# Ten gathered rows moved from ahead of the expert loop to its last quarter, and TensorE's tiles placed at one remainder of 512 bytes

## The chip, the core and the metric

The kernel runs on one core of a Trainium2 chip. The metric is the device time of one execution in microseconds (us). Besides the median of several runs there is one profiled execution, whose trace says when every instruction of every engine started and ended. The engines are named as the profile names them: PE (TensorE's matmuls; PEld are its weight loads), DVE (VectorE), ACT (ScalarE), POOL (GpSimd) and SP, which here only issues DMAs.

## What is computed

One encoder layer over 512 tokens of 1024 values: an input projection, two kinds of attention, an output projection, a layer norm, and then a mixture of 16384 very small experts (PEER) beside a gated embedding. The part that the change moves is PEER:

```python
q   = (xb @ w_q).reshape(128, 8, 256)            # per chunk of 128 tokens
...                                              # two top-16 lists per head, 16 best sums of them
idx = (e1 * 128 + e2).reshape(128, 8 * 16)       # 128 experts per token
g   = softmax(cv)                                # their weights
u   = u_table[idx]                               # 128 x 128 rows of 1024
hpre = einsum('td,ted->te', xb, u)
act  = g * gelu(hpre)
out  = einsum('te,ted->td', act, v_table[idx])
```

## The kernel before

Matmuls of 32-bit values are made from three products: an operand is cut into a high part and a low part (`split`, L103 to L110: ACT copies the high part, DVE subtracts to get the low one), and `mm3` (L120 to L123) adds high x high, high x low and low x high into the same PSUM tile. L121, L122 and L123 are therefore most of TensorE's lines, whatever they compute. In a row of the trace `acc<-v_hi,a_hi` the first operand after the arrow is the one that streams (512 or 256 columns), the second is the one that is loaded as weights (128 columns).

**PEER is done in two ways.** For the first 128 tokens (one per partition) the rows of the two tables are gathered: for each of 128 experts, POOL issues an indirect DMA of 128 rows of 4 KB, and one DVE instruction multiplies them with the tokens and sums (the u rows), or multiplies by a weight and adds to `base` (the v rows). For the other 384 tokens the whole tables go through TensorE: 128 blocks of 128 experts, with a dense weight matrix that is zero except where an expert was chosen.

**Ahead of the loop** (from about 417 us) stand the routing and the building of that matrix. All engines' orders are written out by hand here. DVE's order is the backbone: `route` makes the lists of experts of a chunk of 128 tokens, `build_g` (L887 to L960) makes the weight matrix of a chunk in 16 steps of one-hot masks (`oh`, L936) and weighted masks (`ow_hi`, `ow_lo`, L947), which TensorE multiplies (L914). There are three builds; the last is that of chunk 1 (`build_g(NGC, *held)`, L1202). Among DVE's steps stand gathered rows (`rows`, L962 to L970): 128 u rows of chunk 1 (operand `h_s`) until the second build, then, in the third build, the first `BESIDE` u rows of chunk 0 (L1205, operand `h`); `OWN_G` (L1207) sets how many rows go with a step of the build. Then `SOME` rows of chunk 0 that were fetched ahead, and on to `PRE` (L1315, L1322).

TensorE works there through 104 **lead blocks** (`lead_block`, L1026 to L1042): 512 KB of the u table are loaded (`raw`) and multiplied with 256 tokens (`whole`) in 8 matmuls of plain 32-bit values, each of which the trace shows as two. They are interleaved with DVE's steps by an account: `run_pe` (L878 to L885) adds a step's cost times `PACE` to `due`, and takes so many matmuls of the lead blocks as `due` covers.

**The loop** (L1337 to L1388, from about 918 us) goes over 128 blocks of the v table. Of each block n DVE makes the low part (`v_lo`, or `wlo` for odd n), of each second block also the low part of the weights (`a_lo`) and one product (L1361), and then its share of the gather steps; TensorE does 18 matmuls of 512 columns (`acc`, three chunks x two halves x three products). In the first 22 blocks a further block of the u table goes through TensorE (`expert_in`, 24 products of 256 columns, `hp<-hTh,whi`). Odd blocks from n = 25 keep their parts in a pool of the weights' streams (`whi`, `wlo`), even ones in the loop's own pool (`v_hi`, `v_lo`): that is why their names alternate in the trace. DVE and SP have orders written out by hand in the loop; TensorE's order there is the scheduler's.

`room(n)` (L1326 to L1329) says how many gather steps block n gets, as shares: all 257 steps of chunk 0 (128 u rows, one activation, 128 v rows) less the `PRE` that stand ahead are shared out in proportion.

A tile's place in SBUF follows from the pools: a pool begins where the one below it ends. `even` (L94 to L98) only puts a small tile into a pool so that what comes after it starts further up.

Of the kernel before, what the change touches and what calls it, by code (L numbers as in the profile page):

```python
# [9 lines left out]
F32 = mybir.dt.float32  # L10
# [26 lines left out]
WIDE = 40  # L37
LEAD = 104
SPILL = 72
FIRST = 8  # L40
PACE = 1.07
AHEAD = 14.0
LAG = 6.0
PRE = 41
SOME = 4
EARLY = 15
EARLY_AT = 4
BESIDE = 31
OWN = 1.0
OWN_G = 0.85  # L50
OWN_SOON = 1.2
HALF = 10
OT = 8
# [9 lines left out]
CLOSE = 31  # L63
# [13 lines left out]
def tile_encoder_layer(ctx: ExitStack, tc: tile.TileContext, A: dict, out: bass.AP):  # L77
    nc = tc.nc


    keep = ctx.enter_context(tc.tile_pool(name="keep", bufs=1))
# [9 lines left out]
    eps_t = keep.tile([128, 1], F32, name="eps_t")  # L91
    nc.vector.memset(eps_t, EPS)

    def even(pool):  # L94

        nc.vector.memset(pool.tile([128, 8], F32, name="even"), 0.0)

    even(keep)  # L98

    def r32(ap):  # L100
        return ap.bitcast(F32)
# [70 lines left out]
    turned = pT.enter_context(tc.tile_pool(name="turned", bufs=1, side="right"))  # L172
    hTh = turned.tile([128, 8, T], F32R, name="hTh")
    hTl = turned.tile([128, 8, T], F32R, name="hTl")
    even(turned)


    pA = ExitStack()
    at = pA.enter_context(tc.tile_pool(name="at", bufs=1))
# [17 lines left out]
    gk = at.tile([128, 2], F32, name="gk")  # L197
    ones = at.tile([128, 128], F32, name="ones")
    nc.vector.memset(ones, 1.0)

    def transpose_to(dst_h, dst_l, src, c):

# [445 lines left out]
    pB = ctx.enter_context(tc.tile_pool(name="pB", bufs=1, reuse_waits="tile"))  # L648
# [5 lines left out]
    h_split = None  # L654
    ge_ring = pB.tile([128, GES, 2, N_U], F32, name="ge_ring")
    ge_free = [ge_ring[:, j] for j in range(GES)]
    w_top = pB.tile([128, 2], F32, name="w_top")
    even(pB)

    def expert_in(i):  # L660

# [10 lines left out]
    rt = pR.enter_context(tc.tile_pool(name="rt", bufs=1, reuse_waits="tile"))  # L672
# [20 lines left out]
    v_all = rt.tile([128, 4, 8, 2, 16], F32, name="v_all")  # L693
    i_all = rt.tile([128, 4, 8, 2, 16], U32, name="i_all")
    s_ix = rt.tile([128, 128], I32, name="s_ix")
    even(rt)
    held = []
    rw = pR.enter_context(tc.tile_pool(name="rw", bufs=1, reuse_waits="tile"))
    h_s = rw.tile([128, D], F32, name="h_s")
# [178 lines left out]
    def run_pe(amount):  # L878
        nonlocal due
        due += amount * PACE  # L880
        while due > 0:
# [162 lines left out]
    def on_vector(share, f):  # L1044
        def task():
            nonlocal due
            f()
            due += share * PACE
        return task
# [128 lines left out]
    with tc.manual_schedule(engines={nc.vector.engine, nc.scalar.engine, nc.tensor.engine, nc.sync.engine,  # L1178
# [27 lines left out]
        own_due = 0.0  # L1206
        run(build, OWN_G)  # L1207
        for x in own:
# [27 lines left out]
    for j, (n, nb, _, _) in enumerate(g_tiles[1:], 1):  # L1236
        for c in range(NDC):
            at = n - 6 + c if nb == GB and n < WIDE else n - 4 + c // 2 if n == WIDE else n - 13 + 3 * c
# [65 lines left out]
    with tc.manual_schedule(engines={nc.vector.engine, nc.scalar.engine, nc.tensor.engine, nc.sync.engine,  # L1304
# [14 lines left out]
        for n in range(2):  # L1319
            v_cut[n] = cut_v(n)  # L1320
            blocks_ahead(1)
        for k in range(BESIDE + SOME, PRE):  # L1322
            gather_u(0, k)
        for _ in pe_work:
            pass
    def room(n):  # L1326
        if n < NO_GATHER or n > 124:
            return 0.0
        return 2.2 if n + LEAD < 126 else 1.6 if n < CLOSE else 1.0 if n < WIDE else 1.42 if n < 112 else 1.9  # L1329

    rooms = sum(room(n) for n in range(128))
    done, spent = PRE, 0
    with tc.manual_schedule(engines={nc.vector.engine, nc.sync.engine}):
# [157 lines left out]
```

## Time and profile before

| | |
|---|---|
| median of 3 runs | 1530.96 us (1530.82 to 1531.17) |
| the profiled execution | 1532.45 us |
| its span, first to last instruction | 1530.6 us |
| mean granted TensorE clock | 0.992 |
| instructions | 21801 |

The span is read best in five stretches: the projections and both attentions (0 to about 312 us), the queries and their scores (312 to 417), the lead blocks with routing and builds (417 to about 918), the loop's first blocks with `expert_in` (to about 1075), and the rest of the loop (to about 1519), behind which only the closing layer norms stand. A busy share is a sum over a stretch; since matmuls overlap in the records (one of 512 columns lasts 0.39 us but the next starts some 0.23 us later), what a matmul costs is read from the distance between starts, not from its duration.

### The profile page before, as it was taken

The page shows a single profiled execution, that of the slowest core. Times are in us where ns is not written, and L with a number is a line of the kernel's source. Part 1 is how long each engine was busy: PE and PEld are TensorE (multiplying, and loading weights), DVE is VectorE, ACT ScalarE, POOL GpSimd, SP SyncE. Part 2 cuts the span into 40 slices and gives each one's busy share as a digit, 9 for nine tenths or more (in the row PEclk, how much of TensorE's full clock was granted, in tenths as well). Part 3 has the DMA queues.
Part 4 walks back from the last instruction along what each step waited for, and adds up shares of the span by engine and source line. Part 5 has one row for each costly group of instructions (what it writes and reads, how often), then busy time and mean ns, then how long its engine had stood idle before and what let it go on. Part 6 is the DMA issues. An engine that isn't in the chain of part 4 may idle for free.

```text
span 1530.6 us, 21801 instructions
## 1 busy us (share of the span) xinstructions
PE 1464.4 (96%) x7715; PEld 1221.4 (80%) x7715; DVE 1272.0 (83%) x2639; ACT 543.2 (35%) x893; POOL 626.8 (41%) x537
## 2 busy tenths in 40 slices
PE   6999999999999999999899989999999999999996
PEld 4788777788887788887788878888788888888885
DVE  7276795658999897998889947988788999999998
ACT  3255785333322223222212223443333333333333
POOL 1013110043344344464415345655545555555560
PEclk9999999999999999999999999999999999999999
DMA  7233341194377899999979999999999999999992
GB/s 237 66 107 87 97 125 42 44 304 144 113 234 255 306 400 343 414 399 411 409 298 414 413 387 392 392 395 330 331 391 397 401 398 398 402 395 400 395 347 109
DMA packets 188414, 456.15 MB, mean 298 GB/s; under 512 B 16400, under 2 KB 80272, under 8 KB 185232
## 3 DMA queue, kind: packets, MB, share of 16 engines
q1 hardware_dynamic: 121264, 211.45, 38.6%
q0 software_dynamic: 58400, 208.69, 36.3%
q10 hardware_dynamic: 8640, 34.61, 5.6%
q8 instruction: 61, 1.00, 0.3%
q14 instruction: 49, 0.40, 0.1%
HBM read 413.01 MB, written 38.80 MB: 295 GB/s over the span
## 4 chain that ended last, share of the span: by engine, by line
PE 62%; DVE 13%; issue 10%; DMA 7%; POOL 5%; ACT 1%; SPq 0%; POOLq 0%; DVEq 0%; ACTq 0%
PE acc L121 10%; PE acc L123 10%; PE acc L122 10%; PE mm L1036 5%; DMA raw<-in_uT_dram 4%; PE pj L121 3%; PE pj L122 3%; PE pj L123 3%; PE mm L121 2%; PE mm L123 2%; PE mm L122 2%; POOL whi L966 2%; POOL row L966 2%; POOL wlo L966 2%; PE hp L121 1%
## 5 line engine op out<-in xcount | busy, mean ns | idle before, releaser
L1036 PE MATMUL mm<-whole,raw 128*128 128x256 f32 x1136 | 260.0, 385 | 8.5 <-DMA raw<-in_uT_dram 8.1
L1272 POOL DMA_INDIRECT gat<-in_v_rows_dram,i_sel x128 | 192.3, 1503 | 143.8 <-DVE base L1274 119.9
L1036 PEld LDWEIGHTS mm<-whole,raw 128*128 128x128 f32 x1136 | 213.3, 192 | 40.8 <-DMA raw<-in_uT_dram 7.8
L1257 POOL DMA_INDIRECT gat<-in_u_rows_dram,i_sel x97 | 149.4, 1540 | 119.2 <-DVE gat L1263 91.0
L121 PE MATMUL acc<-v_hi,a_hi 128*128 128x512 f32 x456 | 179.2, 393 | 3.7 <-ACT a_hi L106 2.4
L122 PE MATMUL acc<-v_lo,a_hi 128*128 128x512 f32 x456 | 178.8, 392 | 0.8 <-DVE v_lo L107 0.8
L123 PE MATMUL acc<-v_hi,a_lo 128*128 128x512 f32 x456 | 178.4, 392 | 0.6 <-DVE a_lo L107 0.6
L106 ACT CAST whi<-raw 128x1024 fp32r<-128x1024 f32 (+4 forms) x103 | 102.7, 997 | 199.4 <-PE acc L123 110.1
L1274 DVE SCALAR_TENSOR_TENSOR base<-gat,hdot,base 128x1024 f32<-128x1024 f32 x128 | 165.0, 1289 | 1.8
L107 DVE TENSOR_TENSOR wlo<-raw,whi 128x1024 fp32r<-128x1024 f32 (+4 forms) x103 | 118.6, 1152 | 47.0 <-ACT whi L106 46.2
L106 ACT CAST v_hi<-v_raw 128x1024 fp32r<-128x1024 f32 x76 | 79.8, 1051 | 174.4 <-issue 71.8
L1263 DVE SCALAR_TENSOR_TENSOR gat<-gat,h 128x1024 f32<-128x1024 f32 x97 | 115.0, 1218 | 10.9 <-DMA gat<-in_u_rows_dram,i_sel 10.9
L123 PE MATMUL acc<-whi,a_lo 128*128 128x512 f32 x312 | 123.0, 394 | 0.0
L122 PE MATMUL acc<-wlo,a_hi 128*128 128x512 f32 x312 | 123.0, 394 | 0.0
L121 PE MATMUL acc<-whi,a_hi 128*128 128x512 f32 x312 | 122.5, 394 | 0.0
L107 DVE TENSOR_TENSOR v_lo<-v_raw,v_hi 128x1024 fp32r<-128x1024 f32 x76 | 92.6, 1218 | 28.3 <-ACT v_hi L106 27.8
L121 PEld LDWEIGHTS acc<-v_hi,a_hi 128*128 128x128 f32 x456 | 85.9, 188 | 22.6 <-ACT a_hi L106 2.8
L123 PEld LDWEIGHTS acc<-v_hi,a_lo 128*128 128x128 f32 x456 | 86.0, 189 | 20.1 <-DVE a_lo L107 1.5
L122 PEld LDWEIGHTS acc<-v_lo,a_hi 128*128 128x128 f32 x456 | 86.0, 189 | 18.8 <-DVE v_lo L107 1.1
L966 POOL DMA_INDIRECT row<-in_u_rows_dram,s_ix x42 | 52.7, 1255 | 69.8 <-DVE row L968 44.2
L966 POOL DMA_INDIRECT wlo<-in_u_rows_dram,s_ix x43 | 52.3, 1217 | 68.8 <-DVE wlo L968 55.1
L966 POOL DMA_INDIRECT whi<-in_u_rows_dram,s_ix x43 | 53.9, 1253 | 57.9 <-DVE whi L968 36.9
(395 smaller groups left out, 3370.9 us busy)
## 6 DMA issues: line engine op xcount, KB each, us to landing
raw<-in_uT_dram SPq DMA_DIRECT2D x110, 512.0 KB, 7.4
v_raw<-in_v_rows_dram SPq DMA_DIRECT2D x78, 512.0 KB, 13.1
raw<-in_v_rows_dram SPq DMA_DIRECT2D x50, 512.0 KB, 13.7
g_dram<-g_st ACTq DMA_DIRECT2D x24, 1024.0 KB, 9.5
ge_dram<-ge_ring ACTq DMA_DIRECT2D x36, 256.0 KB, 7.3
g_wide<-g_dram SPq DMA_DIRECT2D x9, 1024.0 KB, 16.8
raw<-in_w_in_dram SPq DMA_DIRECT2D x17, 512.0 KB, 4.0
raw<-in_w_q_dram SPq DMA_DIRECT2D x16, 512.0 KB, 4.3
```

The lines of the kernel that those rows point to most:

```text
L106: nc.scalar.copy(hi, src)
L107: nc.vector.tensor_tensor(lo, src, r32(hi), op=OP.subtract)
L121: nc.tensor.matmul(ps, a[0], b[0], start=start, stop=False)
L122: nc.tensor.matmul(ps, a[0], b[1], start=False, stop=False)
L123: nc.tensor.matmul(ps, a[1], b[0], start=False, stop=stop)
L966: nc.gpsimd.indirect_dma_start(out=u[:np], out_offset=None, in_=u_rows, in_offset=bass.IndirectOffsetOnAxis(ap=ix[:np, k:k + 1], axis=0))
L1036: nc.tensor.matmul(ps[:, :N_U], raw[k], whole[:, k, :], start=(k == 0), stop=(k == 7))
L1257: nc.gpsimd.indirect_dma_start(out=u[:], out_offset=None, in_=u_rows, in_offset=bass.IndirectOffsetOnAxis(ap=i_sel[:, c, k:k + 1], axis=0))
L1263: nc.vector.scalar_tensor_tensor(u, u, 1.0, h[c], op0=OP.mult, op1=OP.mult, accum_out=hdot[:, c, k:k + 1])
L1272: nc.gpsimd.indirect_dma_start(out=u[:], out_offset=None, in_=v_rows, in_offset=bass.IndirectOffsetOnAxis(ap=i_sel[:, c, k:k + 1], axis=0))
L1274: nc.vector.scalar_tensor_tensor(base[c], u, hdot[:, c, k:k + 1], base[c], op0=OP.mult, op1=OP.add)
```

## The change

Three things are changed.

1. **Ten u rows fewer ahead of the loop.** `BESIDE` goes from 31 to 21 and `PRE` from 41 to 31, so the third build has 21 rows beside it and not 31, at a lower share (`OWN_G` from 0.85 to 0.58). `room` gives more steps to blocks 98 to 124. Counted out, the blocks up to 97 get 168 steps as before, blocks 98 to 111 get 28 (before 21) and blocks 112 to 124 get 30 (before 27).
2. **The lead blocks are taken faster**: `PACE` from 1.07 to 1.105. In the program, 69.0 of the 104 lead blocks stood on TensorE ahead of the last product of the second build, now 71.9; ahead of the last product of the third build 98.1, now 98.9.
3. **Tiles are placed differently**: `w_top` goes to another pool, and four small tiles change their size or their pool. Start of a tile in its partition, as the remainder of 512 bytes:

| tiles | before | after |
|---|---|---|
| `hTh`, `hTl`, `w2h`, `w2l`, the NA and the early tiles | 448 | 320 |
| `v_hi`, `v_lo`, `a_hi`, `a_lo`, `whole` | 384 | 320 |
| `g_hi`, `g_lo` | 192 | 320 |
| `whi`, `wlo`, `raw`, `aTh`, `aTl`, `cqh`, `cql`, `ckh`, `ckl` | 320 | 320 |
| `h` and `ident` (transposes only) | 192, 128 | 192, 128 |

```diff
-PACE = 1.07
+PACE = 1.105
-PRE = 41
+PRE = 31
-BESIDE = 31
+BESIDE = 21
-OWN_G = 0.85
+OWN_G = 0.58
...
-    def even(pool):
+    w_top = keep.tile([128, 2], F32, name="w_top")
+
+    def even(pool, n=8):
-        nc.vector.memset(pool.tile([128, 8], F32, name="even"), 0.0)
-    even(keep)
+        nc.vector.memset(pool.tile([128, n], F32, name="even"), 0.0)
...
-    even(turned)
+    even(turned, 40)
...
     nc.vector.memset(ones, 1.0)
+    even(at, 96)
...
-    w_top = pB.tile([128, 2], F32, name="w_top")
-    even(pB)
...
-    even(rt)
+    even(rt, 56)
...
-        return 2.2 if n + LEAD < 126 else 1.6 if n < CLOSE else 1.0 if n < WIDE else 1.42 if n < 112 else 1.9
+        return 2.2 if n + LEAD < 126 else 1.6 if n < CLOSE else 1.0 if n < WIDE else 1.42 if n < 98 else 1.8 if n < 112 else 2.1
```

On DVE, two steps of the third build stood like this before (`row`, `whi` and `wlo` are the buffers that gathered rows go through in turn):

```order
L936 TENSOR_TENSOR oh<-iota,ex 128x2048
L968 SCALAR_TENSOR_TENSOR row,hdot<-row,h_79 128x1024
L947 TENSOR_TENSOR ow_hi<-oh,w_hi 128x1024
L968 SCALAR_TENSOR_TENSOR whi,hdot<-whi,h_79 128x1024
L947 TENSOR_TENSOR ow_lo<-oh,w_lo 128x1024
L936 TENSOR_TENSOR oh<-iota,ex 128x2048
L968 SCALAR_TENSOR_TENSOR wlo,hdot<-wlo,h_79 128x1024
L947 TENSOR_TENSOR ow_hi<-oh,w_hi 128x1024
L968 SCALAR_TENSOR_TENSOR row,hdot<-row,h_79 128x1024
L947 TENSOR_TENSOR ow_lo<-oh,w_lo 128x1024
```

and two steps of it stand like this now:

```order
L936 TENSOR_TENSOR oh<-iota,ex 128x2048
L968 SCALAR_TENSOR_TENSOR whi,hdot<-whi,h_78 128x1024
L947 TENSOR_TENSOR ow_hi<-oh,w_hi 128x1024
L947 TENSOR_TENSOR ow_lo<-oh,w_lo 128x1024
L968 SCALAR_TENSOR_TENSOR wlo,hdot<-wlo,h_78 128x1024
L936 TENSOR_TENSOR oh<-iota,ex 128x2048
L947 TENSOR_TENSOR ow_hi<-oh,w_hi 128x1024
L947 TENSOR_TENSOR ow_lo<-oh,w_lo 128x1024
```

The masks are the same; between them stand fewer rows, about four in three steps where there were two in each.

On DVE in the loop, the pair of blocks 104 and 105 before (`base` is chunk 0's sum, `gat` a gathered row of the v table):

```order
L1361 TENSOR_TENSOR g_wide<-g_wide,ge_ring 128x16x32
L107 TENSOR_TENSOR v_lo<-v_raw,v_hi 128x1024
L107 TENSOR_TENSOR a_lo<-g_wide,a_hi 128x768
L1274 SCALAR_TENSOR_TENSOR base_3252<-gat,hdot,base_3252 128x1024
L107 TENSOR_TENSOR wlo<-raw,whi 128x1024
L1274 SCALAR_TENSOR_TENSOR base_3252<-gat,hdot,base_3252 128x1024 x2
```

and now blocks 104 and 105, then 114 and 115 (L107 has become L108):

```order
L1361 TENSOR_TENSOR g_wide<-g_wide,ge_ring 128x16x32
L108 TENSOR_TENSOR v_lo<-v_raw,v_hi 128x1024
L108 TENSOR_TENSOR a_lo<-g_wide,a_hi 128x768
L1274 SCALAR_TENSOR_TENSOR base_3253<-gat,hdot,base_3253 128x1024 x2
L108 TENSOR_TENSOR wlo<-raw,whi 128x1024
L1274 SCALAR_TENSOR_TENSOR base_3253<-gat,hdot,base_3253 128x1024 x2
...
L1361 TENSOR_TENSOR g_wide<-g_wide,whole 128x16x32
L108 TENSOR_TENSOR v_lo<-v_raw,v_hi 128x1024
L108 TENSOR_TENSOR a_lo<-g_wide,a_hi 128x768
L1274 SCALAR_TENSOR_TENSOR base_3253<-gat,hdot,base_3253 128x1024 x2
L108 TENSOR_TENSOR wlo<-raw,whi 128x1024
L1274 SCALAR_TENSOR_TENSOR base_3253<-gat,hdot,base_3253 128x1024 x3
```

A pair of blocks 98 to 111 has four gather steps where it had three, and from block 112 on mostly five where it had mostly four. What DVE does for TensorE in a pair is the same.

## The prediction

> **What bounds the kernel now.** I read the page first: the share of each engine, the slices over time, the chain that ended last.
>
> ```profile
> PE 1464.4 (96%) x7715; PEld 1221.4 (80%) x7715; DVE 1272.0 (83%) x2639; ACT 543.2 (35%) x893; POOL 626.8 (41%) x537
> ...
> GB/s 237 66 107 87 97 125 42 44 304 144 113 234 255 306 400 343 414 399 411 409 298 414 413 387 392 392 395 330 331 391 397 401 398 398 402 395 400 395 347 109
> ...
> PE 62%; DVE 13%; issue 10%; DMA 7%; POOL 5%; ACT 1%; SPq 0%; POOLq 0%; DVEq 0%; ACTq 0%
> ```
>
> TensorE is busy 96% of the span and most of the chain. From the fifteenth slice on the DMAs move about 400 GB/s. So there are three limits close together, and which of them ends last must be asked stretch by stretch. The windows view answers; its columns are window, length, then busy time of PE, PEld, DVE, ACT and POOL, the granted clock, the DMA share and GB/s.
>
> ```profile
> 312.00:417.00 105.00, 104.96 (x557) 87.52 (x556) 86.22 (x508) 33.82 (x49) 44.08 (x73) 1.00 0.59 191
> 417.00:550.00 133.00, 129.91 (x645) 109.36 (x644) 126.27 (x369) 33.15 (x64) 55.94 (x45) 1.00 0.79 271
> 550.00:738.00 188.00, 176.69 (x1055) 150.87 (x1054) 165.31 (x311) 49.45 (x101) 89.99 (x69) 0.98 1.00 395
> 804.00:886.00 82.00, 77.85 (x544) 68.04 (x543) 74.72 (x112) 23.91 (x51) 40.02 (x32) 1.00 1.02 412
> 886.00:918.00 32.00, 26.03 (x132) 22.31 (x130) 14.00 (x20) 8.38 (x14) 13.34 (x12) 0.95 1.02 386
> 1091.00:1394.00 303.00, 303.00 (x1315) 246.38 (x1314) 275.66 (x290) 104.64 (x111) 170.37 (x113) 1.00 1.03 394
> 1394.00:1502.00 108.00, 108.00 (x470) 87.79 (x469) 102.67 (x96) 36.37 (x38) 57.87 (x39) 1.00 0.95 357
> ```
>
> Ahead of the loop (804 to 918) no engine is full but the DMAs are: TensorE stands 10.1 us of those 114. In the loop from 1091 to 1502 TensorE never stands, DVE has 91% and then 95%, and the DMAs run at 394 and 357 GB/s. A gain there must come from shorter matmuls; a load on DVE there has only 5.3 us of room in the last 108.
>
> **Term 1: TensorE's pace, in the loop.** The timeline of PE at the first matmul of three blocks:
>
> ```profile
> 1203.37 0.39 PE L121 MATMUL acc<-v_hi,a_hi 128*128 128x512 f32 x1
> ...
> 1207.47 0.39 PE L121 MATMUL acc<-whi,a_hi 128*128 128x512 f32 x1
> ...
> 1211.67 0.39 PE L121 MATMUL acc<-v_hi,a_hi 128*128 128x512 f32 x1
> ```
>
> Both blocks have the same 18 matmuls, but the even one takes 4.10 us (228 ns each) and the odd one 4.20 (233 ns). They differ in where the streamed operand lies: `v_hi` at remainder 384 like its weights `a_hi`, `whi` at 320. Two more pairs tell equal remainders from particular ones:
>
> ```profile
> 259.57 0.39 PE L121 MATMUL pj<-whi,aTh 128*128 128x512 f32 x1
> ...
> 261.84 0.39 PE L122 MATMUL pj<-wlo,aTh 128*128 128x512 f32 x1
> ...
> 288.13 0.40 PE L123 MATMUL pj<-w2h,aTl 128*128 128x512 f32 x1
> ...
> 289.99 0.40 PE L122 MATMUL pj<-w2l,aTh 128*128 128x512 f32 x1
> ```
>
> Ten matmuls with both operands at 320 take 2.27 us, 227 ns each; eight with 448 against 320 take 1.86 us, 232.5 ns each. Equal remainders go with 227, at 320 as at 384, unequal ones with 232 to 233. So after the change a block should take 18 x 0.227 = 4.09 us. In blocks 25 to 97 that is 37 odd ones at 0.11 and 36 even ones at 0.01 (these begin slower, behind an odd one): **-4.5 us**, between 0 and -5.
>
> The Trainium skill, "TensorE: Matmul & The Clock Gate", section "Back-to-back issue gap", gives the distance of matmuls by the number of columns alone, about 216 ns for 512, with no word of addresses; by it this term, like 2 and 3, would be nothing, and the sum some 12 us later. The trace has two distances at one number of columns, so I go by the trace and keep the rule as a rival.
>
> **Term 2: the same in the projections and queries.** TensorE is full there (104.96 of 105). The matmuls at 448 against 320 are counted by groups of lines:
>
> ```profile
> L121 PE MATMUL pj<-hTh,whi 128*128 128x512 f32 (+1 forms) x112 | 44.4, 396 | 0.7 <-DVE p_exp L395 0.4 <-DVE rms_ve L334 0.3
> L121 PE MATMUL mm<-hTh,whi 128*128 128x512 f32 (+1 forms) x144 | 53.4, 371 | 0.0
> ```
>
> Each has its like on L122 and L123, so 3 x (112 + 144) = 768, and with 96 each of `w2h` and of the values' projection 960: at 5.5 ns 5.3 us. Some of them stand in the attention, where TensorE also waits for the softmax. I take **-4**, between 0 and -5.3.
>
> **Term 3: the same in the first 22 blocks.**
>
> ```profile
> 1018.23 0.40 PE L121 MATMUL acc<-v_hi,a_hi 128*128 128x512 f32 x1
> ...
> 1022.35 0.28 PE L121 MATMUL hp<-hTh,whi 128*128 128x256 f32 x1
> ...
> 1025.22 0.40 PE L121 MATMUL acc<-v_hi,a_hi 128*128 128x512 f32 x1
> ```
>
> A block takes 4.12 us and its 24 products of 256 columns 2.87, with no gap. The first goes to 4.09. For the second, at 448 against 320, no pair of equal remainders stands in the trace. Bounds: nothing, or the 5.5 ns of the wide ones on each, 0.13 us a block. The extra looked like one per matmul, not per column, so I take most of that: 22 x (0.03 + 0.11) = **-3**, between -0.7 and -3.6.
>
> **Term 4: ten rows fewer beside the third build.** What a row costs DVE (groups of lines), what a lead block costs TensorE (the chain in order of time), and TensorE at the end of the stretch (timeline):
>
> ```profile
> L1263 DVE SCALAR_TENSOR_TENSOR gat<-gat,h 128x1024 f32<-128x1024 f32 x97 | 115.0, 1218 | 10.9 <-DMA gat<-in_u_rows_dram,i_sel 10.9
> ...
> 779.31 23.53 PE mm L1036 x108
> ...
> 895.01 5.41 PE L1036 MATMUL hp<-whole,raw 128*128 128x256 f32 x16 [4.50 <-DMA raw<-in_uT_dram]
> ```
>
> Ten rows are 12.2 us of DVE. They are 10 x 128 x 4 KB = 5.24 MB, at the 412 GB/s of this stretch 12.7 us of the DMAs; the last row shows TensorE waiting 4.50 us for such a transfer. TensorE itself has no row to lose, but `PACE` moves lead blocks ahead: 108 matmuls in 23.53 us are 0.218 each, 16 to a block 3.49 us, and 2.9 blocks more stand ahead of the second build's end (71.9 against 69.0). So behind that point TensorE has 10.1 us less, DVE 12.2, the DMAs 12.7 and the moved blocks' loads besides. All three shrink; the least rules: 10 to 12. What covers the 10 us ahead of that point are TensorE's gaps there, 11.3 us from 550 to 738 and 3.1 from 417. The cover isn't whole: 2.9 blocks are 1.5 MB more, 3.7 us, in a stretch whose DMA share is 1.00 already. I take 11 less 1: **-10**, between -3 and -13.
>
> **Term 5: ten gathers more from block 98 on.** The DVE timeline late in the loop: the end of one pair, the next pair, the block 124; the `v_lo` of block 98, and TensorE at 98 and 124.
>
> ```profile
> 1484.27 2.60 DVE L1274 SCALAR_TENSOR_TENSOR base<-gat,hdot,base 128x1024 f32<-128x1024 f32 x2
> 1486.78 1.22 DVE L107 TENSOR_TENSOR wlo<-raw,whi 128x1024 fp32r<-128x1024 f32 x1
> ...
> 1495.60 1.22 DVE L107 TENSOR_TENSOR wlo<-raw,whi 128x1024 fp32r<-128x1024 f32 x1
> ...
> 1499.85 1.22 DVE L107 TENSOR_TENSOR wlo<-v_raw,whi 128x1024 fp32r<-128x1024 f32 x1
> ...
> 1387.43 1.22 DVE L107 TENSOR_TENSOR v_lo<-v_raw,v_hi 128x1024 fp32r<-128x1024 f32 x1
> ...
> 1394.27 0.39 PE L121 MATMUL acc<-v_hi,a_hi 128*128 128x512 f32 x1
> ...
> 1502.17 0.40 PE L121 MATMUL acc<-whi,a_hi 128*128 128x512 f32 x1
> ```
>
> Two gathers take 2.51 us, so one 1.26; a pair with four takes 8.82, so without them 3.78. At block 98 DVE is 5.6 us ahead of TensorE (1388.65 to 1394.27), at 124 still 1.1: the old order spends its lead just to the end. The new one has 56 gathers in those 13 pairs where there were 46: 13 x 3.78 + 56 x 1.26 = 119.7 us of DVE, against 26 x 4.09 = 106.3 of TensorE. With 6 us of lead, block 124's low part comes 113.7 us behind TensorE's start on 98; before it was 106.8. So **DVE becomes the bound** at about block 114, and the end comes 6.9 us later. Queued behind the gathers on DVE are the next low parts, for which L122 on TensorE waits, and then the closing norms. The new order of TensorE puts high-part products first and leaves five matmuls fewer behind the last low part, 1.1 us: **+6**. Ends: 0, if the lead held, and 12.6, ten gathers in full. The transfers fit: 5.24 MB over 108 us are 49 GB/s, on 357 still under the 412 above; POOL has 58 of 108 us, and ten issues more of 1.5 us are hidden.
>
> ```profile
> L1272 POOL DMA_INDIRECT gat<-in_v_rows_dram,i_sel x128 | 192.3, 1503 | 143.8 <-DVE base L1274 119.9 <-issue 14.3 <-DVE gat L1263 7.4
> ```
>
> The `even` memsets are four of DVE ahead of the first load's landing, and moving `w_top` issues nothing: no cost, and were they bare, under 1 us.
>
> **The sum.** -4.5 - 4 - 3 - 10 + 6 = -15.5, from the profiled execution's 1532.45 us: 1517. That execution lies 1.5 above the median of the runs shown, so the measured time should be near **1515**, with 1510 to 1520 as the forecast's own range.
>
> **Rivals.** *The moved lead blocks pay back ahead of the loop.* The DMAs are full from 550; what is loaded earlier makes DVE's rows and TensorE wait there, and term 4 falls to -3: 1522. For it speaks the DMA share of 1.00, against it TensorE's 14 us of gaps. *The remainder does nothing*, and even and odd blocks differ by something else, such as the pool that DMAs write into: terms 1 to 3 vanish, 1515 + 11.5 = 1527. For it speaks only that I see two remainders equal; against it the 227 ns of `whi,aTh`, from the very pool that is slow in the loop. *DVE keeps up late* because its lead at 98 is larger: 1509. *Slower: a starved TensorE loses its clock.* It has happened once:
>
> ```profile
> 1083.78 0.50 PE L121 MATMUL acc<-v_hi,a_hi 128*128 128x512 f32 x1 [1.24 <-ACT v_hi L106]
> 1085.04 0.49 PE L122 MATMUL acc<-v_lo,a_hi 128*128 128x512 f32 x1 [0.76 <-DVE v_lo L107]
> ...
> 1087.47 0.63 PE L122 MATMUL acc<-v_lo,a_hi 128*128 128x512 f32 x1
> 1087.90 0.63 PE L123 MATMUL acc<-v_hi,a_lo 128*128 128x512 f32 x1
> ```
>
> Behind waits of 2 us the matmuls come 430 ns apart. The Trainium skill, same page, section "What's actually happening", says the clock halves after an idle window of about 3.4 us; the trace shows it behind shorter waits in a row. From block 114 TensorE would wait for each low part. A block at 430 ns takes 7.7 us, 3.2 more than DVE's 4.5; for all twelve that is 38, and 1553. It decides from six such blocks on (19 us). Against it: the waits to come are 0.4 to 0.7 us, and TensorE at half pace never waits, so it should recover.
>
> **How the numbers follow.** A measurement of this kernel tells 0.2%, 3 us, from no change. Forecast 55%, moved blocks pay back 15%, DVE keeps up 12%, remainder nothing 8%, clock 4%; 6% for term 4 and the remainders failing together, about 1531. The range leaves out the last two and most of the fourth: 1506 to 1524. Faster 89%, same 6%, slower 5%.
>
> **What would show it.** Right: odd and even blocks both 4.09 us, `hp<-hTh,whi` under 119 ns apart; the first `acc` near 904 instead of 918; DVE without gaps from block 98, and TensorE waiting on `v_lo` or `wlo` from about 114. Wrong: blocks still 4.10 and 4.20, or all 4.20; more waits on `raw` ahead of 738; a late TensorE without waits, or at half clock.

## The result, and the profile after it

| | before | changed |
|---|---|---|
| median of 7 runs | 1531.17 us (1526.23 to 1532.76) | 1540.17 us (1537.22 to 1545.67) |
| ratio, 95% interval | | 1.0064 (1.0043 to 1.0084) |
| profiled execution | 1532.45 us | 1545.67 us |
| its span | 1530.6 us | 1543.9 us |

The changed kernel is 9 us slower; 15 to 16 us faster was forecast. The profiled execution of the changed kernel is the slowest of its seven, 5.5 us over their median, so its numbers are read by stretch, and two experiments with the same rows are set beside them. Lines of the changed kernel are one higher than before for the split and the matmuls: L107 and L108 are the high and the low part, L122, L123 and L124 the three products.

The page of the changed kernel, the same lines as before: busy time of each engine, and the chain that ended last.

```profile
PE 1461.9 (95%) x7715; PEld 1223.6 (79%) x7715; DVE 1272.5 (82%) x2638; ACT 544.4 (35%) x893; POOL 623.3 (40%) x537
...
PE 43%; DVE 21%; DMA 18%; issue 11%; POOL 3%; ACT 2%; SPq 1%; DVEq 0%; POOLq 0%; ACTq 0%
```

TensorE has fallen from 62% to 43% of the chain, DVE has risen from 13% to 21% and the DMAs from 7% to 18%. The windows view says where. It is asked by blocks of the loop: 40 to 75, 76 to 97, 98 to 111, 112 to 123 (columns as in the prediction). Before:

```profile
1153.60:1303.00 149.40, 149.40 (x650) 121.49 (x649) 135.33 (x135) 51.45 (x55) 83.23 (x56) 1.00 1.04 399
1303.00:1394.30 91.30, 91.30 (x398) 74.26 (x397) 84.23 (x79) 31.31 (x33) 51.06 (x35) 1.00 1.04 399
1394.30:1452.40 58.10, 58.10 (x254) 47.23 (x253) 53.73 (x51) 19.97 (x21) 32.25 (x23) 1.00 1.04 396
1452.40:1502.20 49.80, 49.80 (x218) 40.50 (x217) 48.84 (x46) 16.41 (x17) 25.32 (x17) 1.00 0.85 312
```

The changed kernel:

```profile
1144.90:1291.80 146.90, 146.90 (x650) 121.63 (x649) 132.21 (x145) 50.72 (x54) 87.41 (x56) 1.00 1.04 399
1291.80:1387.10 95.30, 91.56 (x397) 73.70 (x396) 85.24 (x80) 32.59 (x34) 48.84 (x34) 1.00 1.04 398
1387.10:1452.60 65.50, 58.64 (x253) 46.78 (x252) 59.31 (x55) 19.88 (x21) 41.55 (x28) 0.99 1.04 396
1452.60:1514.20 61.60, 55.83 (x217) 44.34 (x218) 59.05 (x54) 16.27 (x17) 32.20 (x22) 0.90 0.83 294
```

Up to block 76 the change gains, though less than the some 20 us that terms 1 to 4 have up to there: that block begins 11.2 us earlier (1291.8 against 1303.0). Then each stretch loses: 4.0, 7.4 and 11.8 us. The first of these is known only roughly: in three experiments whose instructions are the changed kernel's up to block 98, blocks 76 to 97 take 92.5 to 97.6 us. The last two columns show a split that I had averaged away: from block 40 to 111 the DMAs have a share of 1.04 and move 396 to 399 GB/s in both kernels, while behind block 112 their share is only 0.83 to 0.85. What ACT waited for between 1091 and 1500 us (waits view: total, times, longest), before and after:

```profile
ACT v_hi L106 <- DMA v_raw<-in_v_rows_dram: 19.0, 5, 7.2
ACT whi L106 <- DMA raw<-in_v_rows_dram: 8.5, 4, 3.8
```

```profile
ACT whi L107 <- DMA raw<-in_v_rows_dram: 79.4, 24, 10.0
ACT v_hi L107 <- DMA v_raw<-in_v_rows_dram: 47.1, 21, 9.9
```

The blocks of the v table land late, 126.5 us of ACT's waiting instead of 27.5. The longest of the `v_hi` waits ends at TensorE (timelines of ACT and PE):

```profile
1450.81 1.04 ACT L107 CAST v_hi<-v_raw 128x1024 fp32r<-128x1024 f32 x1 [9.92 <-DMA v_raw<-in_v_rows_dram]
1451.76 0.83 ACT L107 CAST a_hi<-g_wide 128x768 fp32r<-128x768 f32 x1
```

```profile
1452.64 0.79 PE L122 MATMUL acc<-v_hi,a_hi 128*128 128x512 f32 x1 [5.63 <-ACT a_hi L107]
```

TensorE's wait is put down to ACT's `a_hi` of block 112. DVE had made the product for it at 1445.8, but in ACT's order it stands behind the `v_hi` of block 114, which waited 9.92 us for its load, and it starts as that one ends. So a late load of block 114 already holds TensorE at block 112.

Behind block 112 it looks different (timelines of DVE, ACT and PE):

```profile
1467.29 3.97 DVE L1274 SCALAR_TENSOR_TENSOR base<-gat,hdot,base 128x1024 f32<-128x1024 f32 x3
1471.18 0.68 DVE L1361 TENSOR_TENSOR g_wide<-g_wide,whole 128x512 f32<-128x512 f32 x1
```

```profile
1472.82 0.83 ACT L107 CAST a_hi<-g_wide 128x768 fp32r<-128x768 f32 x1
```

```profile
1473.69 0.73 PE L122 MATMUL acc<-v_hi,a_hi 128*128 128x512 f32 x2 [1.91 <-ACT a_hi L107]
```

Here no DMA is late. DVE's product L1361, from which ACT makes `a_hi`, stands behind three gathers (3.97 us), and TensorE's first matmul of the block waits for it. So there are two theories for the late loss: **A**, the DMAs at their cap, and **B**, DVE; and **C** for what is lost around the loop's start, `PACE`.

### The profile page after: what moved, and what is told of

Its sections match the earlier page's. It is cut to its first block, busy times and chain, and to the rows that moved or that the text cites. A ratio compares the mean times of both kernels' runs of the same rounds, so it can differ in the third digit from the quotient of the medians.

```text
span 1543.9 us, 21820 instructions
## 1 busy us (share of the span) xinstructions
PE 1461.9 (95%) x7715; PEld 1223.6 (79%) x7715; DVE 1272.5 (82%) x2638; ACT 544.4 (35%) x893; POOL 623.3 (40%) x537
## 4 chain that ended last, share of the span: by engine, by line
PE 43%; DVE 21%; DMA 18%; issue 11%; POOL 3%; ACT 2%; SPq 1%; DVEq 0%; POOLq 0%; ACTq 0%
PE mm L1036 10%; DMA raw<-in_uT_dram 5%; DMA raw<-in_v_rows_dram 5%; DMA v_raw<-in_v_rows_dram 4%; DVE base L1274 3%; PE pj L122 3%; PE pj L124 3%; PE pj L123 3%; PE acc L122 3%; PE acc L123 3%; PE acc L124 3%; DMA gat<-in_u_rows_dram,i_sel 2%; PE mm L122 2%; DVE gat L1263 2%; PE mm L124 2%
## 5 line engine op out<-in xcount | busy, mean ns | idle before, releaser
L1257 POOL DMA_INDIRECT gat<-in_u_rows_dram,i_sel x107 | 165.5, 1547 | 133.4 <-DVE gat L1263 99.2
L122 PE MATMUL acc<-v_hi,a_hi 128*128 128x512 f32 x456 | 181.4, 399 | 20.4 <-ACT a_hi L107 20.1
L124 PE MATMUL acc<-v_hi,a_lo 128*128 128x512 f32 x456 | 181.1, 400 | 2.9 <-DVE a_lo L108 2.5
L123 PE MATMUL acc<-v_lo,a_hi 128*128 128x512 f32 x456 | 180.5, 397 | 0.8 <-DVE v_lo L108 0.8
L107 ACT CAST whi<-raw 128x1024 fp32r<-128x1024 f32 (+4 forms) x103 | 102.7, 997 | 178.1 <-DMA raw<-in_v_rows_dram 87.7
L108 DVE TENSOR_TENSOR wlo<-raw,whi 128x1024 fp32r<-128x1024 f32 (+4 forms) x103 | 118.7, 1152 | 52.4 <-ACT whi L107 52.1
L1263 DVE SCALAR_TENSOR_TENSOR gat<-gat,h 128x1024 f32<-128x1024 f32 x107 | 127.0, 1218 | 12.8 <-DMA gat<-in_u_rows_dram,i_sel 12.8
L107 ACT CAST v_hi<-v_raw 128x1024 fp32r<-128x1024 f32 x76 | 79.8, 1051 | 146.3 <-DMA v_raw<-in_v_rows_dram 70.8
L124 PE MATMUL acc<-whi,a_lo 128*128 128x512 f32 x312 | 121.4, 389 | 0.0
L123 PE MATMUL acc<-wlo,a_hi 128*128 128x512 f32 x312 | 121.0, 389 | 0.0
L122 PEld LDWEIGHTS acc<-v_hi,a_hi 128*128 128x128 f32 x456 | 87.4, 192 | 41.2 <-ACT a_hi L107 23.2
L122 PE MATMUL acc<-whi,a_hi 128*128 128x512 f32 x312 | 118.3, 389 | 0.0
L108 DVE TENSOR_TENSOR v_lo<-v_raw,v_hi 128x1024 fp32r<-128x1024 f32 x76 | 92.5, 1218 | 26.7 <-ACT v_hi L107 26.3
L124 PEld LDWEIGHTS acc<-v_hi,a_lo 128*128 128x128 f32 x456 | 87.5, 192 | 26.7 <-DVE a_lo L108 7.5
L123 PEld LDWEIGHTS acc<-v_lo,a_hi 128*128 128x128 f32 x456 | 87.7, 192 | 18.7 <-DVE v_lo L108 1.1
L925 ACT ACTIVATE g_st<-tr 128x512 f32<-128x512 f32 x96 | 52.7, 595 | 65.8 <-PE tr L914 47.9
```

What stands on the lines that cost most here:

```text
L107: nc.scalar.copy(hi, src)
L108: nc.vector.tensor_tensor(lo, src, r32(hi), op=OP.subtract)
L122: nc.tensor.matmul(ps, a[0], b[0], start=start, stop=False)
L123: nc.tensor.matmul(ps, a[0], b[1], start=False, stop=False)
L124: nc.tensor.matmul(ps, a[1], b[0], start=False, stop=stop)
L925: nc.scalar.mul(stage[:, :, x:x + 4], ps.rearrange("p (t i) -> p i t", t=4), 1.0 if c == NGC else 1.0 / W_MAX)
```

## Experiments

Ratios are to the kernel before, run beside each; its median was 1529.5 to 1530.7 us.

### The parts of the change, one by one

**Places only** (the numbers of before):

```diff
-PACE = 1.105
+PACE = 1.07
-PRE = 31
+PRE = 41
-BESIDE = 21
+BESIDE = 31
-OWN_G = 0.58
+OWN_G = 0.85
-... 1.42 if n < 98 else 1.8 if n < 112 else 2.1
+... 1.42 if n < 112 else 1.9
```

> Only the tiles' places are changed; PACE, PRE, BESIDE, OWN_G and room are those of before. Theory A, the DMAs are already at their cap in the loop (share 1.04, about 400 GB/s, both before and after the change, blocks 40 to 112): matmuls of odd blocks come 227 ns apart wherever TensorE runs, but a block's loads and gathers still take 4.15 us, so TensorE's gain is given back in waits on v_hi, a_hi or raw; about 3 us faster than before (between 0 and 6), and block 98 begins no more than 4 us earlier. The theory of the prediction, TensorE alone sets the pace from block 25 to 112: 4.08 us a block throughout and 7 to 9 us faster than before, no new waits.

Measured: 1525.5 us, ratio 0.9971 (0.9957 to 0.9985), 5.2 us under the kernel before. The windows for blocks 76 to 97, 98 to 111 and 112 to 123:

```profile
1293.60:1384.40 90.80, 90.33 (x398) 74.17 (x397) 81.16 (x77) 31.20 (x33) 49.98 (x34) 1.00 1.04 398
1384.40:1441.50 57.10, 57.10 (x253) 47.23 (x252) 53.40 (x51) 20.91 (x22) 32.03 (x22) 1.00 1.04 396
1441.50:1494.00 52.50, 50.75 (x218) 40.15 (x216) 52.04 (x49) 15.98 (x17) 28.32 (x19) 1.00 0.89 337
```

Theory A was too strict: but for 1 us in blocks 76 to 97 TensorE keeps its 4.08 us a block up to 112 (block 98 begins 9.9 us earlier, not 4), with the DMAs at 1.04 throughout. The stock of loads ahead pays for it: at block 98 the low part is ready 0.6 us ahead (`v_lo` ends at 1383.8, the block begins at 1384.4) where it was 5.6, and without that lead the last twelve blocks cost 2.7 us more than before.

**Numbers only** (the places of before): the diff above the other way round, on the kernel before.

> Only the numbers (PACE, PRE, BESIDE, OWN_G, room) are changed; all tiles stay where they were before. Theory A (DMA cap in the loop): the ten rows gain about 10 us at the loop's start, lose some 7 at the loop's first blocks, and the seven rows more in blocks 98 to 111 cost 7 x 0.52 MB at 400 GB/s, about 9 us, and the three of the last blocks some more: 5 to 12 us slower than before, so that all of the loss is in the numbers. Theory of the prediction (terms 4 and 5, DVE as the only late bound): about 4 us faster than before. If the loss came from the places instead (faster matmuls that starve and lose their clock), this run would be as fast as before or faster.

Measured: 1546.67 us, ratio 1.0106 (1.0082 to 1.0130), 16 us slower; its blocks 98 to 111 take 63.4 us and 112 to 123 62.0. The loss is in the numbers, more than I expected, and the places take some 6 us off it.

**The changed kernel with the old PACE:**

```diff
-PACE = 1.105
+PACE = 1.07
```

> The changed kernel with PACE back at 1.07. Theory C, the 7 us lost in blocks 2 to 4 come from lead blocks whose loads were moved forward: the loss at the loop's entry goes, and the time is 4 to 7 us under the changed kernel. Theory A: the entry loses what it does because the loop's first loads meet full DMAs whenever it starts earlier; PACE moves nothing of that, and the time is within 3 us of the changed kernel.

Measured: 1536.33 us, ratio 1.0037 (1.0021 to 1.0052), 3.8 us under the changed kernel: just short of theory C's 4 to 7, and more than theory A's 3.

**Places and the new PACE**, all rows as before:

```diff
-PACE = 1.07
+PACE = 1.105
```

> The places of the change and PACE 1.105, all rows where they were before. Theory C, PACE's moved lead blocks cost 4 to 7 us in the loop's first blocks: 2 to 6 us slower than the places alone, with block 0 no later but block 6 later by that much, since the rows beside the third build are as many as before. If the loss at the loop's entry came from starting the loop earlier (fewer rows), it doesn't occur here, and the time is that of the places alone.

Measured: 1531.39 us, ratio 1.0008 (0.9997 to 1.0020), 5.9 us over the places alone. So `PACE` costs 4 to 6 us in both pairs, with the rows of before and with the change's. The first DVE instruction of the third build, `w_lo`, in the places alone, the changed kernel with the old `PACE`, the changed kernel, and the places with the new `PACE`:

```profile
799.59 0.42 DVE L905 SCALAR_TENSOR_TENSOR w_lo<-tr,w_hi 128x256 f16<-128x256 f32 x1 [2.40 <-ACT ex L899]
```

```profile
801.14 0.42 DVE L905 SCALAR_TENSOR_TENSOR w_lo<-tr,w_hi 128x256 f16<-128x256 f32 x1 [1.33 <-ACT w_hi L904]
```

```profile
813.48 0.42 DVE L905 SCALAR_TENSOR_TENSOR w_lo<-tr,w_hi 128x256 f16<-128x256 f32 x1 [8.20 <-ACT w_hi L904]
```

```profile
807.73 0.42 DVE L905 SCALAR_TENSOR_TENSOR w_lo<-tr,w_hi 128x256 f16<-128x256 f32 x1 [6.44 <-ACT ex L899]
```

With 1.07 DVE waits 1.3 to 2.4 us there (3.7 before the change), with 1.105 it waits 6.4 to 8.2; over all runs of this document it is 1.3 to 3.7 and 3.8 to 10.2. It waits for ACT, and ACT for transposes on TensorE (`tr`, L893), ahead of which more lead blocks now stand (timelines of PE and ACT in the changed kernel):

```profile
794.72 17.43 PE L1036 MATMUL mm<-whole,raw 128*128 128x256 f32 x80
```

```profile
812.51 0.65 ACT L899 CAST ex<-tr 128x256 f16<-128x256 f32 x2 [3.83 <-PE tr L893]
```

The blocks taken earlier are paid back by DVE, and at the loop's start by a late load, which term 4 below shows.

**A lower PACE still** (places, `PACE = 1.04`):

> The places of the change with PACE 1.04 instead of 1.07, all rows as before. PACE 1.105 makes DVE wait 6 to 8 us for w_lo at the start of the third build (1.3 to 3.7 us with 1.07), because the transposes ahead of it stand behind more lead blocks on TensorE. If that wait is the whole of PACE's effect, 1.04 takes away the rest of it, up to 2 us, and the time is 0 to 2 us under the places alone; if the lead blocks left behind the build then come later than what they save, it is 1 to 4 us over the places alone.

Measured: 1539.86 us, ratio 1.0071 (1.0052 to 1.0089), 14 us over the places alone. Both expectations fell. `w_lo` waits 5.4 us here too, and the lead blocks left over run into a load just ahead of the loop:

```profile
897.39 2.07 PE L1036 MATMUL hp<-whole,raw 128*128 128x256 f32 x4 [8.29 <-DMA raw<-in_uT_dram]
```

Block 0 begins at 930.6 us, 16 later than with the places alone. Why 1.04 costs so much wasn't followed further; of the three values tried, 1.07 is the best.

**The old room** for the changed kernel:

```diff
-... 1.42 if n < 98 else 1.8 if n < 112 else 2.1
+... 1.42 if n < 112 else 1.9
```

> The changed kernel with the shares of room as before, so that the ten moved rows are spread: 54, 16, 11, 94, 23 and 28 steps in blocks 0-21, 22-30, 31-39, 40-97, 98-111 and 112-124 (changed kernel 52, 15, 10, 91, 28, 30; before 51, 16, 10, 91, 21, 27). Theory A: blocks 98 to 111 get 5 rows fewer (about 6 us there), blocks 40 to 97 three more (about 4 us given back there); with two rows fewer behind that 4 to 7 us under the changed kernel. Theory B, DVE's overload in the last blocks with the clock that TensorE loses there makes the whole loss: with 28 steps instead of 30 there and 23 instead of 28 ahead, the time falls to 10 us or more under the kernel before, 15 to 20 under the changed one.

Measured: 1532.97 us, ratio 1.0013 (0.9996 to 1.0031), 7.2 us under the changed kernel, theory A's number (4 to 7). Blocks 98 to 111 take 58.5 us and 112 to 123 52.2; blocks 76 to 97, with more rows now, 97.2.

### DMAs or DVE

**Half the bytes behind block 98**, DVE's work unchanged:

```diff
+        if k >= 70:
+            nc.gpsimd.indirect_dma_start(out=u[:, 0:512], out_offset=None,
+                                         in_=v_rows.rearrange("r (a b) -> (r a) b", a=2), ...)
+            b2 = base[c].rearrange("p (a b) -> p a b", a=2)
+            nc.vector.scalar_tensor_tensor(b2, u[:, 0:512].unsqueeze(1).to_broadcast([128, 2, 512]), ...)
```

> The changed kernel, but from block 98 on each v gather loads only half a row (2 KB instead of 4 KB, another half row than the reference's), and DVE's instruction reads that half twice, so that DVE works as long as before: 58 gathers move 15 MB instead of 30. Theory A, the DMAs bound blocks 98 to 111: with about 7 MB less there those 14 blocks take 58 to 61 us instead of 65.5, what is left being DVE's own 61.7 less its lead; with some lead kept, blocks 112 to 123 fall from 61.6 to 56 to 58; in all 8 to 12 us under the changed kernel. Theory B, DVE bounds them: it works as long as before, so 98 to 111 stay at 62 to 65 us, 112 to 123 at 60 to 62, and the time is within 3 us of the changed kernel.

**Half of DVE's gather work behind block 98**, the bytes unchanged:

```diff
-        nc.vector.scalar_tensor_tensor(base[c], u, hdot[:, c, k:k + 1], base[c], ...)
+        m = D // 2 if k >= 70 else D
+        nc.vector.scalar_tensor_tensor(base[c][:, :m], u[:, :m], hdot[:, c, k:k + 1], base[c][:, :m], ...)
```

> The changed kernel, but from block 98 on DVE weighs and adds only half of each gathered v row (512 of 1024 values; the other half of those rows is left out of the result), at about 0.7 us instead of 1.26, while the DMAs load whole rows. Theory A: blocks 98 to 111 still ask for 1.89 MB each, 4.7 us at 397 GB/s, and stay at 62 to 66 us; only 112 to 123, where DVE is the bound, fall from 61.6 to about 50: 10 to 14 us under the changed kernel. Theory B: with DVE at half its gather time both stretches go back to TensorE's own 57 and 49 us, and the time is 18 to 22 us under the changed kernel.

**Both halves at once:**

> The changed kernel, but from block 98 on each gather loads only half a row (another half row than the reference's) and DVE works only on that half; the rest of those rows is left out. Theory A and B each for its own stretch (DMAs for blocks 98 to 111, DVE for 112 to 123; each half alone freed only one of the two): both stretches are freed at once, 57 to 58 and 49 to 51 us, no late loads behind block 124 as with DVE's half alone, and the time is 17 to 22 us under the changed kernel, 8 to 12 under the kernel before. If a third thing holds the late blocks (the clock, TensorE's order), it is less than 12 us under the changed kernel.

Measured: 1534.67 us (ratio 1.0026, 1.0013 to 1.0038), 1537.51 (1.0051, 1.0033 to 1.0069) and 1517.69 (0.9928, 0.9906 to 0.9950). The windows for blocks 98 to 111 and 112 to 123, with half the bytes:

```profile
1386.40:1444.10 57.70, 57.48 (x254) 47.21 (x252) 57.23 (x54) 20.11 (x21) 40.51 (x28) 1.00 0.87 291
1444.10:1505.20 61.10, 54.06 (x217) 42.17 (x215) 57.43 (x52) 16.28 (x18) 34.20 (x23) 0.94 0.63 198
```

With half of DVE's work, and a third row for what follows up to the last blocks:

```profile
1381.10:1446.60 65.50, 60.55 (x254) 49.14 (x253) 48.74 (x60) 19.76 (x21) 34.65 (x30) 0.95 1.04 398
1446.60:1497.40 50.80, 49.11 (x217) 40.32 (x215) 37.92 (x47) 15.46 (x17) 24.48 (x21) 1.00 0.91 363
1497.40:1514.60 17.20, 11.87 (x36) 8.62 (x37) 12.72 (x19) 4.30 (x5) 0.00 (x0) 0.70 0.18 62
```

With both:

```profile
1381.60:1438.70 57.10, 57.10 (x253) 47.31 (x252) 52.05 (x64) 19.70 (x21) 39.43 (x32) 1.00 0.96 346
1438.70:1487.70 49.00, 49.00 (x217) 40.56 (x217) 40.52 (x51) 17.77 (x19) 24.39 (x19) 1.00 0.66 220
```

A table of two by two: fewer bytes take the first stretch from 65.5 to 57.7 and leave the second (61.1, was 61.6); less work on DVE leaves the first at 65.5 and takes the second to 50.8. **So the DMAs bound blocks 98 to 111, and DVE bounds 112 to 123.** Neither alone brings back what its stretch shows, and neither total came out as expected: with half the bytes only 5.5 us are gained (8 to 12 expected under A), with half of DVE's work only 2.7 (10 to 14). In the latter the 36 matmuls from block 124 on take 17.2 us, where the changed kernel's take 8.1. ACT waits there for loads again:

```profile
1494.67 1.05 ACT L107 CAST v_hi<-v_raw 128x1024 fp32r<-128x1024 f32 x1 [8.53 <-DMA v_raw<-in_v_rows_dram]
...
1502.17 1.04 ACT L107 CAST v_hi<-v_raw 128x1024 fp32r<-128x1024 f32 x1 [4.77 <-DMA v_raw<-in_v_rows_dram]
```

These are the parts of blocks 126 and 127, and those of 124 and 125 stand behind them in ACT's order. The DMAs move 109 GB/s from 1490 to 1497 us and 62 in that row, so for the second of these loads at least it is not their cap that makes it late; what does was not followed. With both freed the two stretches are TensorE's own, 57.1 and 49.0, and 22.5 us are gained.

**Half the bytes ahead of block 98** (the first 70 v gathers, the same edit with `k < 70`):

> The changed kernel, but the first 70 v gathers (blocks 52 to 97) load half a row each (another half row than the reference's) and DVE reads that half twice, so that its work stays: 18 MB less for the DMAs ahead of block 98, nothing changed behind it. Theory A, the DMAs at about 400 GB/s take back in blocks 76 to 97 what TensorE has gained: those 22 blocks take TensorE's own 89.8 us instead of 95.3, DVE's low part at block 98 is 5 to 7 us ahead instead of 2, loads are ahead too, blocks 98 to 111 take 58 to 62 us instead of 65.5, and the time is 10 to 15 us under the changed kernel. If the waits in 76 to 97 are not the DMAs' (DVE or the order of the issues), those blocks and the time stay within 3 us of the changed kernel.

Measured: 1528.39 us, ratio 0.9992 (0.9979 to 1.0005), 11.8 us under the changed kernel. Blocks 76 to 97, 98 to 111, 112 to 123:

```profile
1288.90:1378.60 89.70, 89.70 (x397) 74.30 (x396) 83.84 (x79) 31.36 (x33) 54.63 (x34) 1.00 0.91 320
1378.60:1436.30 57.70, 57.35 (x254) 47.14 (x252) 55.45 (x52) 20.19 (x21) 38.74 (x26) 1.00 1.03 384
1436.30:1496.20 59.90, 51.64 (x217) 39.83 (x217) 57.94 (x53) 16.14 (x18) 32.20 (x22) 1.00 0.89 325
```

Theory A's numbers. Behind block 98 nothing was taken away, and yet 98 to 111 fall to 57.7: the low part of block 98 is 6.7 us ahead (ready at 1372.0, the block begins at 1378.6), and with loads ahead the stretch lives on stock. The last stretch stays at 59.9 with a clock of 1.00, so it is DVE's time, not the clock's.

### Where the rows can go

If the loop is full from block 40 on, rows may still fit into blocks 6 to 21, where the DMAs move 369 GB/s at a share of 1.00 and DVE has 96.7 of 111.9 us before the change:

```profile
962.30:1074.20 111.90, 111.90 (x675) 100.06 (x674) 96.68 (x130) 45.07 (x57) 65.06 (x41) 1.00 1.00 369
```

Four kernels with the places of the change and `PACE` 1.07 tried it (steps in blocks 0 to 21; 112 to 124; the rest as before but for one or two):

| rows fewer ahead of the loop | steps 0 to 21 (before 51) | steps 112 to 124 (before 27) | us, ratio (interval) |
|---|---|---|---|
| 0 | 55 | 24 | 1527.30, 0.9983 (0.9972 to 0.9994) |
| 3 | 58 | 25 | 1528.15, 0.9992 (0.9979 to 1.0005) |
| 6 | 58 | 25 | 1526.04, 0.9974 (0.9960 to 0.9988) |
| 10 | 60 | 27 | 1522.36, 0.9952 (0.9937 to 0.9966) |

> The places of the change, the numbers of before, and room 2.4 instead of 2.2 for blocks 1 to 21 and 1.7 instead of 1.9 behind block 111: 55, 16, 10, 90, 21 and 24 steps in blocks 0-21, 22-30, 31-39, 40-97, 98-111 and 112-124 (before 51, 16, 10, 91, 21, 27). In blocks 6 to 21 the DMAs move only 364 to 369 GB/s at a share of 0.99 and DVE stands some 15 us, so under theory A the four steps more cost nothing there, and three gathers fewer at 1.26 us give DVE back the 3 us that it costs at the end with the places alone: 3 us (1 to 4) under the run with the places alone. If the DMAs of blocks 0 to 21 have no room either, the same time as with the places alone, or above it.

> The places of the change with PACE 1.07, three rows fewer ahead of the loop (PRE 38, BESIDE 28, OWN_G 0.77), and more rows in blocks 6 to 21: 12, 46, 15, 10, 90, 21 and 25 steps in blocks 0-5, 6-21, 22-30, 31-39, 40-97, 98-111, 112-124 (before 13, 38, 16, 10, 91, 21, 27). Theory A: the loop starts 2 to 3 us earlier, blocks 6 to 21 have room for eight rows more (DVE stands 15 us of 112 there, the DMAs move 365 GB/s), and two late gathers fewer give 1 to 2 us: 2 to 5 us under the places alone, the fastest of all. If blocks 6 to 21 have no room (the run with four rows more in blocks 0 to 21 gave no gain), the same time as the places alone or more.

> The same with six rows fewer ahead of the loop (PRE 35, BESIDE 25, OWN_G 0.69): 13, 45, 16, 10, 91, 22 and 25 steps in the same stretches. If the place makes the loss: 1 to 4 us under the places alone. If the number makes it: as the places alone, or 1 to 3 us over them.

> The places of the change, PACE 1.07, the ten rows fewer ahead of the loop as in the change (PRE 31, BESIDE 21, OWN_G 0.58), but the ten rows put into blocks 6 to 21: 13, 47, 17, 10, 90, 22 and 27 steps in blocks 0-5, 6-21, 22-30, 31-39, 40-97, 98-111 and 112-124 (before 13, 38, 16, 10, 91, 21, 27). If the place of the rows makes the loss (DMAs and DVE full behind block 40, some 30 GB/s left in blocks 6 to 21): the loop begins 7 us earlier as with the change's rows at PACE 1.07, blocks 6 to 21 give 1 to 3 us of it back, the rest stays as with the places alone: 2 to 6 us under the places alone, 1519 to 1524 us. If their number makes it (the DMAs are full from 550 us on, so the ten rows cost some 13 us wherever they stand): as slow as the change's rows at PACE 1.07, 5 us over the kernel before.

The edit of the last:

```diff
-PRE = 41
+PRE = 31
-BESIDE = 31
+BESIDE = 21
-OWN_G = 0.85
+OWN_G = 0.58
-        return 2.2 if n + LEAD < 126 else 1.6 if n < CLOSE else 1.0 if n < WIDE else 1.42 if n < 112 else 1.9
+        return 2.2 if n < 6 else 2.65 if n + LEAD < 126 else 1.65 if n < CLOSE else 1.0 if n < WIDE else 1.4 if n < 112 else 1.9
```

With zero, three and six rows I missed: none beats the places alone (1525.5). Blocks 112 to 123 were freed (49.0, 50.9 and 49.5 us; 52.5 with the places alone), but the loop didn't begin where it should: at 917.1, 916.3 and 915.5 us, not ahead of the 914.5 of the places alone. The places alone and the first of this table have the same instructions up to the loop and yet differ by 2.6 us there: single profiles differ by as much as these rows are worth. **With ten rows it holds**: 1522.36 us, 7 to 8 us under the kernel before and 14 under the same ten rows put late with the same `PACE` (1536.33). Its windows for blocks 6 to 21, 98 to 111 and 112 to 123:

```profile
951.20:1062.90 111.70, 111.70 (x674) 100.11 (x673) 100.79 (x140) 44.20 (x56) 79.22 (x48) 1.00 1.03 389
...
1383.00:1440.10 57.10, 57.10 (x254) 47.28 (x253) 53.59 (x51) 20.18 (x22) 33.45 (x22) 1.00 1.04 396
1440.10:1493.00 52.90, 50.82 (x218) 39.96 (x216) 52.24 (x49) 15.99 (x18) 28.31 (x19) 1.00 0.90 333
```

Nine more rows in blocks 6 to 21 cost no time there, 111.7 us as without them. So, beside `PACE`, it was the place of the rows, not their number, that lost the time. This is the fastest of the kernels that do all of the work; it is 3 us under the places alone, with intervals that overlap.

## Why the prediction was wrong

**Term 1, right.** Odd and even blocks take 4.08 us each (timeline of PE in the changed kernel, three blocks in a row):

```profile
1197.95 0.39 PE L122 MATMUL acc<-whi,a_hi 128*128 128x512 f32 x1
...
1202.03 0.39 PE L122 MATMUL acc<-v_hi,a_hi 128*128 128x512 f32 x1
...
1206.11 0.39 PE L122 MATMUL acc<-whi,a_hi 128*128 128x512 f32 x1
```

18 matmuls at 227 ns. With the places alone, blocks 25 to 97 took 298.9 us instead of 303.0: -4.1 for a forecast of -4.5. The rival that the remainder does nothing has fallen. That equal remainders decide was tested only with all tiles at 320.

**Term 2, half.** The first matmul of the lead blocks starts at 414.6 instead of 416.6 us: -2, not -4.

**Term 3, wrong.** Products of 256 columns gain nothing. One block's 24 of them, from the first to the next `acc`:

```profile
961.45 0.28 PE L122 MATMUL hp<-hTh,whi 128*128 128x256 f32 x1
...
964.32 0.40 PE L122 MATMUL acc<-v_hi,a_hi 128*128 128x512 f32 x1
```

2.87 us, as before with unequal remainders. Of two bounds I took the upper one on the ground that the extra looked like one per matmul; it isn't.

**Term 4, too large, and a rival came true with it.** -10 was forecast, and the loop's first matmul did come 12.1 us earlier (905.7 against 917.9, 2 of it term 2), but 7.2 us of it are gone by block 5, which begins only 4.9 earlier (950.4 against 955.3). Most of that is one wait of TensorE, again behind a load for which ACT waits (timelines of ACT and PE):

```profile
936.50 1.04 ACT L107 CAST v_hi<-v_raw 128x1024 fp32r<-128x1024 f32 x1 [7.69 <-DMA v_raw<-in_v_rows_dram]
...
939.95 0.82 ACT L107 CAST a_hi<-g_near 128x768 fp32r<-128x768 f32 x1
```

```profile
940.82 0.80 PE L122 MATMUL acc<-v_hi,a_hi 128*128 128x512 f32 x1 [5.56 <-ACT a_hi L107]
```

All seven runs with `PACE` 1.105 and the ten rows fewer have such a wait there, of 4.7 to 7.9 us; the two with 1.07 and as few rows have none over 1 us in the loop's first blocks. Taken apart at block 6: the places alone 4.7 us earlier, the rows with the old `PACE` 5.3 more, and `PACE` alone 3.8 later with the rows of before, 5.0 with the change's. These are single profiles: in four experiments with the changed kernel's instructions up to there, block 6 begins at 952.9 to 955.4 us instead of 957.3, so each of these figures can be off by some 4 us. As far as that goes, the rows are worth about 5, not 10, and `PACE`, which the step used to explain why TensorE has less left to do, took back most of that. This is the rival "the moved lead blocks pay back ahead of the loop", and its number: less the 2 us of term 2, block 6 is 3 us earlier. Its DVE wait is there, but for TensorE's transposes; the wait for loads that I argued comes only at the loop's start. Why a higher `PACE` makes these loads late was not followed.

**Term 5, the step that failed.** Blocks 98 to 123 were forecast at 113.2 us (106.3 + 6.9) and took 127.1, 125.2 with the old `PACE` and 125.4 with the old places: 17 to 19 us more than the 107.9 before, not 6. Two sentences of it were wrong. "The transfers fit" set 49 GB/s on a mean of 357 and compared with 412. But the mean was of 396 GB/s at a share of 1.04 up to block 111 and 312 behind it, and 412 came from another stretch with other transfers. The seven rows added to blocks 98 to 111 are 3.67 MB, at 396 GB/s 9.3 us; 65.5 less TensorE's 57.1 is 8.4. And "with 6 us of lead": the DMAs had no room for a TensorE that asks for the same bytes 1.7% sooner, so the lead was used up on the way. At block 98 the changed kernel had 2.0 us of it:

```profile
1383.99 1.21 DVE L108 TENSOR_TENSOR v_lo<-v_raw,v_hi 128x1024 fp32r<-128x1024 f32 x1
```

```profile
1387.15 0.39 PE L122 MATMUL acc<-v_hi,a_hi 128*128 128x512 f32 x1
```

DVE as the bound behind block 112 was right, and its price of 1.26 us a gather too; what was missing is that it began there with nothing in hand: the wait of 5.6 us at block 112 held DVE's next step too.

The DMA share of 1.03 stood in the prediction's own quote for 1091 to 1394 us, and I used it for a stretch ahead of the loop but not there. The Trainium skill, "DMA: Bandwidth & Descriptors", section "Where 436 GB/s comes from", says that HBM to SBUF transfers are bound by about 358 GB/s of the HBM side, with 435 as the fabric's ceiling. The trace stands between: 396 to 399 GB/s for 300 us at a share of 1.04, so the cap that counts here is the one measured in the loop itself.

**The clock rival.** The clock was 0.90 in blocks 112 to 123 and the kernel did become slower, but not for that reason: the same stretch takes 59.9 us at a clock of 1.00 with half the bytes ahead, so by these two runs the clock is worth 1.7 us of the 11.8 at most.

**The sum**, in the profiled executions: -4.9 at block 6, -2.3 to block 98 (the places' 5.2 less 3 for late loads), +7.4, +11.8, and +1.3 from block 124 on: 13.3 us of span. The forecast had -14.8 at block 6 (terms 2 and 4, and six of the 22 blocks of term 3), -6.7 from there to block 98 and +6 behind it. So of the 28.8 us between the forecast and this profile 9.9 were lost ahead of block 6, 4.4 on the way to 98, and 14.5 behind it: term 5 is half of the miss, and a third was lost ahead of block 6, most of it in term 4.

## What to carry to other kernels

Where an engine and the DMAs were both full, as here, making the engine faster first ate the stock of loads ahead and only later showed as waits; ask what the DMAs move in that very stretch, at what share, and how many bytes a block needs. A mean over a stretch with two limits fits nothing: cut it where the share changes before saying that a transfer fits. Work that is to be moved goes where both its engine and its bytes have room, here into blocks 6 to 21 and not to the end.

## What the runs showed of the hardware that was not expected

- The distance between the matmuls of 512 columns (tiles of type fp32r) went with both operands' start in the partition: 227 ns at equal remainders of 512 bytes (320 or 384 for both), 232 to 233 at unequal ones (448 against 320, 320 against 384). With 256 columns it is 120 ns either way (2.87 us for 24).
- One core's DMAs held 396 to 399 GB/s at a share of 1.04 for hundreds of us with half of the bytes from gathers of 4 KB rows (58 of 119 MB in blocks 40 to 111 before the change); a share of 1.00 with 369 GB/s in blocks 6 to 21 still had room for 389.
- TensorE's clock fell to 0.90 in blocks 112 to 123, behind a wait of 5.6 us and with three more of 2 us in it, and cost at most 1.7 us there (61.6 us against 59.9 at 1.00 with half the bytes ahead), where DVE set the pace.
